# Swapping the stationary and the moving operand in the up, q/k/v and query products of a two-layer decoder trunk

## The chip, the cores and the metric

The kernel runs on one core of one Trainium2 chip. The metric is the device time of one execution in microseconds (us), as the median over several runs. A second number, the span, comes from one execution taken by the hardware profiler. Engines are named as the profile names them: PE is the matrix engine TensorE and PEld its weight loads, DVE is VectorE, ACT is ScalarE, POOL is GpSimd, and SP is the engine whose queue issues the weight transfers.

## The reference

x has 256 tokens of 2048 features, in float32. The trunk has two layers:

- Layer 1 is gated DeltaNet. `p = x @ w_in` gives q, k, v, a gate z and two scalars per head (16 heads of 128). A causal convolution of four taps and SiLU run over the tokens of each q/k/v channel; q and k are normalised per head, and a chunked delta rule (with a triangular solve) gives the heads' outputs, which are normalised, gated by SiLU(z) and multiplied by `w_out`.
- Layer 2 is differential attention. One product of the stream with `shared_w_kv` gives k and v; `x @ w_q` gives two query sets per head; the head's weights are softmax(1) - lambda * softmax(2); the result is normalised and multiplied by `w_o`.
- Each layer ends with an MLP, `square(relu(x @ w_up)) @ w_down`, with 8192 hidden features. After each of the four sub-layers comes `x <- LayerNorm(alpha * x + f(x))`.

Nearly all of the arithmetic is in the products of x (256 rows) with float32 weights, 421 MB of them in all, each read once.

## The kernel before

**Number format.** A float32 operand is split into a high and a low part of the type float32r: `split` (lines 77 to 79) copies the source into the high part on ScalarE (L78) and subtracts it on VectorE (L79). A product is then three matmuls, high x high, high x low and low x high, accumulated in PSUM (`product`, L174 to L176).

**Tiling of a product.** All big products go through `gemm`, which only puts an entry into a list, and `run`, which works the list off. A product of 1024 output columns (`C`) is cut along the depth into steps of four blocks of 128 (`SC`). For each depth block one transfer on SP's queue brings 128 rows of 1024 weights (512 KB, L159), and one split makes `wh` and `wl`. Inside a step, the kernel goes over two token tiles `t` of 128 tokens, over the depth blocks, and over two groups of 512 columns (`G`). The stationary operand is a 128 x 128 block of x (depth by tokens, `x_stat` or `act_stat`), the moving operand is 512 columns of weights, and the result is a PSUM bank of [128 tokens, 512 features]. After the first token tile of a step, the loads of the next step are emitted (L148 to L150), and after each token tile `pump` emits some units of queued head work.

**Transposes.** The next operation wants its operand with features on the partitions. So the evacuation of an up product (`up`, L341 to L350) takes Relu and square into a tile `sm` and queues `to_features` with `soon`. `run` takes one queued entry behind each depth block (L141 to L144): four transposes of 128 x 128 on TensorE (`transpose4`, L204), then a split out of PSUM. In the DeltaNet, q, k and v are evacuated into `sm` (L693), transposed and copied (`channels`, L499), since the convolution runs along the tokens of a channel. In the attention, `heads` does the same for k and q (L794, L798).

**Layout of x.** `xhl` (L61) holds x by features, as [128, part, token tile, depth block, 128 tokens].

**Order of the work.** The list is DeltaNet (k, q, v for the first eight heads, then for the others, two gate products, two output products), MLP, attention (k and q for the first eight heads, then for the others, two v products, two output products), MLP. An MLP goes through its 8192 hidden features in four quarters of 2048: two up products, then two down products onto the residual. Units of head work (convolutions, scores, the steps of the triangular inverse) are emitted by `pump` between the matmuls, in the order in which they were queued. After a LayerNorm the first products are cut [6, 5, 5] instead of [4, 4, 4, 4].

**Buffers.** Four raw weight tiles, six high and six low ones, eleven blocks of [128, 2048] (`blk`), eight small tiles (`sm`), and eight PSUM banks: four accumulators (`acc`) and four for everything else (`ps`).

## Time and profile before

| | |
|---|---|
| time, median of 3 runs | 2463.02 us (2461.49 to 2467.75) |
| time of the profiled execution | 2465.03 us |
| its span | 2463.3 us, mean clock of TensorE 0.992 |
| weight transfers on SP's queue | 420.79 MB, 52.0% of 16 DMA engines over the span |
| HBM read | 433.70 MB, 177 GB/s over the span |
| matmuls of 512 columns into `acc` | 9600 (3 lines x 3200) |
| transposes on L204 | 512 of `sm` tiles, 128 of `blk` tiles |

How to read a group row: line, engine, operation, output <- inputs, shape, count | busy time and mean duration of one in ns | idle time of that engine just before them, and what ended most of it. A row of a timeline is start, duration (both in us from the span's start), engine, line, operation, operands, count. A matmul's duration overlaps that of its neighbours, so the rate at which matmuls run is seen from their starts.

### The profile page before, as it was taken

Reading aid. Unit: us, or ns where it says so; the run is one execution under the profiler, and the core shown is the slowest. Engines: PE = TensorE matmul, PEld = TensorE weight load, DVE = VectorE, ACT = ScalarE, POOL = GpSimd, SP = SyncE. Lnnn points to the kernel's source line nnn. Section 1 sums busy time; section 2 is a strip of 40 time slices with the busy share of each in tenths; the row PEclk is TensorE's granted clock in tenths of the full one; section 3 lists DMA queues with packets and bytes.
Section 4 is the critical chain, followed back from the end, with each engine's and each line's share of the span. In section 5 each row is a group of like instructions: output and inputs, shape, how many; then the busy total and the mean of one; then the engine's idle time right before and its main releaser. Section 6 shows DMA issues by size and latency. Waiting matters only on the chain.

```text
span 2463.3 us, 30465 instructions
## 1 busy us (share of the span) xinstructions
PE 2416.1 (98%) x11492; PEld 1983.3 (81%) x11492; DVE 1497.2 (61%) x2333; ACT 1078.2 (44%) x1474; POOL 90.3 (4%) x94
## 2 busy tenths in 40 slices
PE   8999999998999999999998999999999999999997
PEld 7888888887888888888887878788788888888886
DVE  4789689667554544545557575665755554555556
ACT  4545345433443433434433464643443443443442
POOL 0010010002000000000002000000200000000001
PEclk9999899999999999999999999999999999999999
DMA  6545345564555556565554545455455555656553
GB/s 229 155 139 175 98 140 160 166 233 158 188 185 191 182 194 222 172 214 182 195 197 146 180 137 171 155 174 167 161 198 195 182 190 186 217 179 214 185 195 121
DMA packets 120211, 438.84 MB, mean 178 GB/s; under 512 B 13760, under 2 KB 13792, under 8 KB 119040
## 3 DMA queue, kind: packets, MB, share of 16 engines
q1 hardware_dynamic: 115920, 420.79, 52.0%
q0 software_dynamic: 2560, 11.13, 1.4%
q10 hardware_dynamic: 1584, 4.98, 0.5%
q8 instruction: 90, 1.47, 0.2%
q14 instruction: 57, 0.47, 0.1%
HBM read 433.70 MB, written 3.15 MB: 177 GB/s over the span
## 4 chain that ended last, share of the span: by engine, by line
PE 90%; DVE 6%; DMA 2%; issue 1%; ACT 1%; POOL 0%; ACTq 0%; POOLq 0%; DVEq 0%
PE acc L174 27%; PE acc L175 27%; PE acc L176 27%; PE ps L204 3%; DVE wl L79 1%; DVE blk L266 1%; DVE blk L265 1%; PE ps L819 1%; ACT wh L78 1%; PE ps L550 1%; DMA wr<-in_gdn_w_in_dram 1%; PE ps L485 1%; DMA wr<-in_mlp_w_up_dram 0%; PE ps L621 0%; PE ps L847 0%
## 5 line engine op out<-in xcount | busy, mean ns | idle before, releaser
L79 DVE TENSOR_TENSOR wl<-wr,wh 128x1024 fp32r<-128x1024 f32 x785 | 954.5, 1227 | 675.0 <-ACT wh L78 632.1
L78 ACT CAST wh<-wr 128x1024 fp32r<-128x1024 f32 x800 | 832.1, 1052 | 945.6 <-PE acc L176 757.2
L174 PE MATMUL acc<-wh,xhl 128*128 128x512 f32 x1920 | 764.3, 398 | 0.0
L175 PE MATMUL acc<-wl,xhl 128*128 128x512 f32 x1920 | 757.7, 395 | 3.2 <-POOL wl L79 3.2
L176 PE MATMUL acc<-wh,xhl 128*128 128x512 f32 x1920 | 754.8, 393 | 0.0
L174 PE MATMUL acc<-wh,blk 128*128 128x512 f32 x1280 | 500.0, 391 | 0.0
L176 PE MATMUL acc<-wh,blk 128*128 128x512 f32 x1280 | 499.4, 390 | 0.0
L175 PE MATMUL acc<-wl,blk 128*128 128x512 f32 x1280 | 499.1, 390 | 0.0
L175 PEld LDWEIGHTS acc<-wl,xhl 128*128 128x128 f32 x1920 | 363.7, 189 | 75.7 <-POOL wl L79 4.4
L174 PEld LDWEIGHTS acc<-wh,xhl 128*128 128x128 f32 x1920 | 363.8, 189 | 73.8 <-issue 1.7
L176 PEld LDWEIGHTS acc<-wh,xhl 128*128 128x128 f32 x1920 | 362.7, 189 | 73.9
L176 PEld LDWEIGHTS acc<-wh,blk 128*128 128x128 f32 x1280 | 240.4, 188 | 50.1
L174 PEld LDWEIGHTS acc<-wh,blk 128*128 128x128 f32 x1280 | 240.4, 188 | 49.5
L175 PEld LDWEIGHTS acc<-wl,blk 128*128 128x128 f32 x1280 | 240.5, 188 | 49.2
L293 DVE SCALAR_TENSOR_TENSOR blk<-blk,acc 128x512 f32<-128x512 f32 x80 | 54.7, 685 | 85.2 <-PE acc L176 85.2
L204 PE MATMUL ps<-ident,sm 128*128 128x128 f32 x512 | 81.3, 275 | 2.5 <-DVE sm L869 1.8
L204 PEld LDWEIGHTS ps<-ident,sm 128*128 128x128 f32 x512 | 61.3, 140 | 27.3 <-PE acc L176 7.1
L78 ACT CAST blk<-ps 128x512 fp32r<-128x512 f32 x80 | 46.8, 585 | 70.9 <-PE ps L204 70.9
L347 DVE TENSOR_TENSOR sm<-sm 128x512 f32<-128x512 f32 x64 | 44.0, 691 | 52.6 <-ACT sm L346 52.2
L79 DVE TENSOR_TENSOR blk<-ps,blk 128x512 fp32r<-128x512 f32 x80 | 55.0, 688 | 30.1 <-ACT blk L78 30.1
L346 ACT ACTIVATE sm<-acc 128x512 f32<-128x512 f32 x64 | 38.2, 597 | 65.4 <-PE acc L176 62.4
L471 DVE SCALAR_TENSOR_TENSOR sm<-blk,g_cw,sm 128x255 f32<-128x255 f32 (+2 forms) x144 | 60.8, 474 | 0.0
(202 smaller groups left out, 1049.7 us busy)
## 6 DMA issues: line engine op xcount, KB each, us to landing
wr<-in_mlp_w_up_dram SPq DMA_DIRECT2D x256, 512.0 KB, 4.7
wr<-in_mlp_w_down_dram SPq DMA_DIRECT2D x256, 512.0 KB, 5.2
wr<-in_gdn_w_in_dram SPq DMA_DIRECT2D x128, 512.0 KB, 4.4
wr<-in_shared_w_kv_dram SPq DMA_DIRECT2D x64, 512.0 KB, 5.1
wr<-in_gdn_w_out_dram SPq DMA_DIRECT2D x32, 512.0 KB, 5.4
wr<-in_diff_w_q_dram SPq DMA_DIRECT2D x32, 512.0 KB, 4.6
wr<-in_diff_w_o_dram SPq DMA_DIRECT2D x32, 512.0 KB, 4.7
blk<-in_ln_g_dram POOLq DMA_DIRECT2D x4, 1024.0 KB, 7.2
```

The costliest lines, as they stand in the source:

```text
L78: self.nc.scalar.copy(hi, src)
L79: (engine or self.nc.vector).tensor_tensor(lo, src, hi.bitcast(F32), op=ALU.subtract)
L174: mm(ps, xh, wh[:, c], start=(k == 0), stop=False)
L175: mm(ps, xh, wl[:, c], start=False, stop=False)
L176: self.last = mm(ps, xl, wh[:, c], start=False, stop=(k == nk - 1))
L204: self.nc.tensor.transpose(pt[:, i], src[:, i * P : (i + 1) * P], self.ident)
L265: v.scalar_tensor_tensor(xc, xc, ln["mv", t][:, 0:1], ln["g"][:, c], op0=ALU.subtract, op1=ALU.mult)
L266: v.scalar_tensor_tensor(xc, xc, ln["rs", t], ln["b"][:, c], op0=ALU.mult, op1=ALU.add)
L293: self.nc.vector.scalar_tensor_tensor(rc, rc, alpha, ps, op0=ALU.mult, op1=ALU.add)
L346: self.nc.scalar.activation(a, ps, AF.Relu)
L347: self.nc.vector.tensor_tensor(a, a, a, op=ALU.mult)
L471: v_.scalar_tensor_tensor(y[:, i, d:], u[:, : T - d], w(j), y[:, i, d:], op0=ALU.mult, op1=ALU.add)
```

## The change

Three families of products change their operands: up (all but the first 1024 columns of each MLP, which stay since they follow a LayerNorm), the DeltaNet's q/k/v, and the attention's queries and the second half of its keys. They go through a new list entry, `features`, of 512 output features. Now a 128 x 128 block of weights (depth by features) is stationary, x moves in passes of 256 columns (all tokens), and the result arrives as [128 features, 256 tokens]: four such blocks fill a pair of PSUM banks. No transposes follow; Relu, square and split (or the plain copies of q/k/v) work on the block as it is. Down, gate, v and output products stay as they were.

What goes with it: `xhl` and the activations become [128, depth block, part, 256 tokens], so that both token tiles stand next to each other; a weight transfer brings two depth blocks of 512 columns (runs of 2 KB) instead of one of 1024 (runs of 4 KB); a step covers eight depth blocks, with the same four transfers; the accumulators become two pairs of banks.

```diff
-        self.acc = pool("acc", 4, space=PSUM)
+        self.acc = pool("acc", 2, space=PSUM)
...
-        self.xhl = self.const.tile([P, 2, NT, KD, P], F32R, name="xhl")
+        self.xhl = self.const.tile([P, KD, 2, T], F32R, name="xhl")
...
+    def features(self, w, c0, evac, pre=None, rate=1):
+        wsrc = lambda k: w[k * P : (k + 2) * P, c0 : c0 + G].rearrange("(k p) c -> p k c", p=P)
+        self.plan.append((KD, wsrc, None, evac, pre, rate, None, [2 * SC] * (KD // (2 * SC))))
...
+            if stat is None:
+                if s == 0:
+                    acc = self.acc.tile([P, NG, G], F32, name="acc")
+                self.feature_passes(acc, ws, evac if s + n >= nk else None, lambda: self.load_next(loaded, steps, j), rate)
+                continue
...
+    def feature_passes(self, acc, ws, evac, load, rate):
+        blocks = acc.rearrange("p g (b t) -> p (g b) t", t=T)
+        mm = self.nc.tensor.matmul
+        for n, (k0, wh, wl) in enumerate(ws):
+            for i in range(2):
+                k = k0 + i
+                xh, xl = self.xhl[:, k, 0], self.xhl[:, k, 1]
+                for b in range(4):
+                    c = slice(i * G + b * P, i * G + (b + 1) * P)
+                    mm(blocks[:, b], wh[:, c], xh, start=(k == 0 and b % 2 == 0), stop=False, skip_group_check=True)
+                    mm(blocks[:, b], wh[:, c], xl, start=False, stop=False, skip_group_check=True)
+                    self.last = mm(
+                        blocks[:, b], wl[:, c], xh, start=False, stop=(k == KD - 1 and b % 2 == 1), skip_group_check=True
+                    )
+                if k != ws[0][0] and self.pending:
+                    fn, args = self.pending.popleft()
+                    with self.after(self.last):
+                        fn(*args)
+            if n == len(ws) // 2 - 1:
+                load()
+                self.pump(rate)
+        if evac is not None:
+            evac(blocks)
+        self.pump(rate)
...
-        for k in range(s, s + n):
+        for k in range(s, s + n, 2 if pairs else 1):
             wr = self.raw.tile([P, C], F32, name="wr")
-            self.nc.sync.dma_start(wr, wsrc(k))
+            self.nc.sync.dma_start(wr.rearrange("p (k c) -> p k c", k=2) if pairs else wr, wsrc(k))
...
-            if k == 0:
-                acc[g, t] = self.acc.tile([P, G], F32, name="acc")
+            if k == 0 and g == 0:
+                pair = self.acc.tile([P, NG, G], F32, name="acc")
+                acc.update({(i, t): pair[:, i] for i in range(NG)})
...
+            def up_features(blocks, h=h):
+                h.append(self.blk(F32R))
+                hv = self.act_view(h[-1])
+                a = [self.sm() for _ in range(2)]
+                for i in range(2):
+                    self.nc.scalar.activation(a[i], blocks[:, 2 * i : 2 * i + 2], AF.Relu)
+                for i in range(2):
+                    self.nc.vector.tensor_tensor(a[i], a[i], a[i], op=ALU.mult)
+                for i in range(2):
+                    kb = slice(2 * i, 2 * i + 2)
+                    self.split(hv[:, kb, 0], hv[:, kb, 1], a[i].rearrange("p (k q) -> p k q", k=2))
...
-            for n in range(FQ // C):
-                self.gemm(
-                    KD, self.cols(w_up, f * FQ + n * C), self.x_stat, up(n), cuts=[6, 5, 5] if f == n == 0 else None
-                )
+            first = C if f == 0 else 0
+            if first:
+                self.gemm(KD, self.cols(w_up, 0), self.x_stat, up(0), cuts=[6, 5, 5])
+            for c0 in range(first, FQ, G):
+                self.features(w_up, f * FQ + c0, up_features)
...
-            def ev_for(name, ct):
-                def ev(gi, t, ps):
-                    if (gi, t) == (0, 0):
+            def ev_for(name, ct, u):
+                def ev(blocks):
+                    if u == 0:
                         hf["raw"] = self.blk().rearrange("p (h t) -> p h t", h=HH)
-                    a = self.sm()
-                    nc.scalar.copy(a, ps)
-                    if (gi, t) == (NG - 1, NT - 1):
-                        turned(gi, t, a)
-                    else:
-                        self.soon(turned, gi, t, a)
...
+                    for h in (0, 2):
+                        nc.scalar.copy(hf["raw"][:, u * 4 + h : u * 4 + h + 2], blocks[:, h : h + 2])
+                    if u == 1:
                         follow()
...
-                self.gemm(KD, self.cols(w_in, c0 + H * DK), self.x_stat, ev_for(name, ct + H), pre=pre, rate=2)
+                for u in range(2):
+                    self.features(
+                        w_in, c0 + H * DK + u * G, ev_for(name, ct + H, u), pre=pre if u == 0 else None, rate=2
+                    )
...
-            return heads("q", follow)
+            for u in range(2):
+                self.features(w_q, hh * C + u * G, head_features("q", u, follow))
...
-            self.gemm(KD, self.cols(w_q, hh * C), self.x_stat, q_heads(hh))
+            if hh == 0:
+                self.gemm(KD, self.cols(w_kv, 0), self.x_stat, heads("k"), pre=constants, cuts=[6, 5, 5])
+            else:
+                for u in range(2):
+                    self.features(w_kv, C + u * G, head_features("k", u))
+            q_heads(hh)
```

`head_features` copies a block's four feature blocks into the heads' tile on ScalarE, as `ev` does for q/k/v. The gate scalars of the DeltaNet (L425, L426) read the new layout of x in the same matmuls.

More of the change, by code (lines that the diff above doesn't have):

```diff
@@ L147, in run, with load_next @@
                             evac(g, t, acc[g, t])
-                if t == 0 and j + 1 < len(steps):
-                    with self.after(self.hold):
-                        self.load_weights(loaded, *steps[j + 1], self.hold is not None)
-                    self.hold = None
+                if t == 0:
+                    self.load_next(loaded, steps, j)
                 self.pump(rate)
+    def load_next(self, loaded, steps, j):
+        if j + 1 < len(steps):
+            with self.after(self.hold):
+                self.load_weights(loaded, *steps[j + 1], self.hold is not None)
+            self.hold = None
@@ L161, in load_weights @@
             wl = self.lo.tile([P, C], F32R, name="wl")
-            self.split(wh, wl, wr, self.nc.gpsimd if share and k % 2 else None)
+            self.split(wh, wl, wr, self.nc.gpsimd if share and (k - s) // (2 if pairs else 1) % 2 else None)
             ws.append((k, wh, wl))
@@ L232, in turn @@
             with self.after(self.last):
-                self.to_features(r[t][:, cut(q)], self.xhl[:, :, :, q * 4 : q * 4 + 4], t)
+                self.to_features(r[t][:, cut(q)], self.xhl[:, q * 4 : q * 4 + 4], t)
         for c in (cut(0), slice(G, D)):
@@ L267, in ln_apply @@
         if ln["out"] is None:
-            self.to_features(xc, self.xhl[:, :, :, q * 4 : q * 4 + 4], t)
+            self.to_features(xc, self.xhl[:, q * 4 : q * 4 + 4], t)
         else:
@@ L420, in gates @@
             pg = self.ps()
[L421 removed]
+            pv2 = pg.rearrange("p (s q) -> p s q", s=2)
             for k in range(KD):
[L423 removed]
+                xk = self.xhl[:, k]
                 c = slice(k * P, (k + 1) * P)
[L425 to L426 removed]
+                nc.tensor.matmul(pv2, wh[:, c], xk, start=(k == 0), stop=False, skip_group_check=True)
+                nc.tensor.matmul(pv2[:, 0], wl[:, c], xk[:, 0], start=False, stop=(k == KD - 1), skip_group_check=True)
             gt = self.sm()
@@ L799, in turned, with head_features, ev @@
                 if follow is not None and (gi, t) == (NG - 1, NT - 1):
+                    follow()
+            return ev
+        def head_features(name, u, follow=None):
+            def ev(blocks):
+                if u == 0:
+                    st[name] = self.blk().rearrange("p (h t) -> p h t", h=8)
+                for h in (0, 2):
+                    nc.scalar.copy(st[name][:, u * 4 + h : u * 4 + h + 2], blocks[:, h : h + 2])
+                if follow is not None and u == 1:
                     follow()
```

24 lines of the change are left out of this document (6 added, 18 removed).

## The prediction

> **What bounds the kernel now.** I read the page first: engine shares, then the chain that ended last, then the costliest groups.
>
> ```profile
> span 2463.3 us, 30465 instructions
> ...
> PE 2416.1 (98%) x11492; PEld 1983.3 (81%) x11492; DVE 1497.2 (61%) x2333; ACT 1078.2 (44%) x1474; POOL 90.3 (4%) x94
> ...
> PE 90%; DVE 6%; DMA 2%; issue 1%; ACT 1%; POOL 0%; ACTq 0%; POOLq 0%; DVEq 0%
> ...
> L79 DVE TENSOR_TENSOR wl<-wr,wh 128x1024 fp32r<-128x1024 f32 x785 | 954.5, 1227 | 675.0 <-ACT wh L78 632.1
> L78 ACT CAST wh<-wr 128x1024 fp32r<-128x1024 f32 x800 | 832.1, 1052 | 945.6 <-PE acc L176 757.2
> L174 PE MATMUL acc<-wh,xhl 128*128 128x512 f32 x1920 | 764.3, 398 | 0.0
> ...
> L174 PE MATMUL acc<-wh,blk 128*128 128x512 f32 x1280 | 500.0, 391 | 0.0
> ...
> L204 PE MATMUL ps<-ident,sm 128*128 128x128 f32 x512 | 81.3, 275 | 2.5 <-DVE sm L869 1.8
> ...
> L78 ACT CAST blk<-ps 128x512 fp32r<-128x512 f32 x80 | 46.8, 585 | 70.9 <-PE ps L204 70.9
> L347 DVE TENSOR_TENSOR sm<-sm 128x512 f32<-128x512 f32 x64 | 44.0, 691 | 52.6 <-ACT sm L346 52.2
> L79 DVE TENSOR_TENSOR blk<-ps,blk 128x512 fp32r<-128x512 f32 x80 | 55.0, 688 | 30.1 <-ACT blk L78 30.1
> L346 ACT ACTIVATE sm<-acc 128x512 f32<-128x512 f32 x64 | 38.2, 597 | 65.4 <-PE acc L176 62.4
> ```
>
> TensorE is the bound: 90% of the chain, and its big matmuls idle 0.0 us before them. ScalarE (L78) and VectorE (L79), which split the weights, wait for TensorE (757.2 us of L78's idle time) and not the other way round. But a busy share says nothing of how long one matmul holds the engine, since neighbours overlap (398 ns each times 1920 is far more than their share). For that I cut one quarter of the last MLP (two up products of 1024 columns, then two down products of 1024) at its product borders and asked each stretch for its transposes alone; the columns are the stretch, its length, TensorE busy in L204 (count), weight loads (count), clock, DMA share, GB/s.
>
> ```profile
> 1915.28:1960.29 45.01, 1.82 (x12) 1.41 (x12) 1.00 0.57 187
> 1960.29:2005.80 45.51, 2.42 (x16) 1.90 (x16) 1.00 0.56 185
> 2005.80:2049.82 44.02, 0.60 (x4) 0.49 (x4) 1.00 0.59 192
> 2049.82:2093.34 43.52, 0.00 (x0) 0.00 (x0) 1.00 0.59 194
> ```
>
> The fourth product has no transpose and takes 43.52 us for its 192 matmuls of 512 columns (16 blocks of depth, 2 token tiles, 2 column groups, 3 terms): **226.7 ns each**, at the full clock. The other three exceed 43.52 by 1.49, 1.99 and 0.50 us and hold 3, 4 and 1 groups of four transposes. So 3.98 us over 8 groups: **0.497 us per group**, and nothing else in the quarter costs TensorE anything. The single events agree (start, duration):
>
> ```profile
> 628.38 0.39 PE L176 MATMUL acc<-wh,xhl 128*128 128x512 f32 x1
> 628.61 0.60 PE L204 MATMUL ps<-ident,sm 128*128 128x128 f32 x4
> 628.96 0.48 PE L174 MATMUL acc<-wh,xhl 128*128 128x512 f32 x1
> 629.28 0.40 PE L175 MATMUL acc<-wl,xhl 128*128 128x512 f32 x1
> 629.51 0.39 PE L176 MATMUL acc<-wh,xhl 128*128 128x512 f32 x1
> ```
>
> From L176 to the second matmul behind the group pass 0.90 us, 0.45 more than two matmuls; the rest of the 0.497 is in the following ones (here 0.23 instead of 0.227).
>
> **Which work is changed.** A block of 512 output features by 256 tokens was 96 matmuls of 512 columns (16 depths, 2 token tiles, 3 terms) and becomes 192 of 256 (16 depths, 4 feature blocks, 3 terms). Blocks that change: up, 14 in each of two MLPs (16 less the first 1024 columns) = 28; q/k/v of the DeltaNet, 6 products of 2 = 12; query products 2 of 2 = 4; the second key product 2. Together 46. So 4416 matmuls of 512 columns become 8832 of 256, the streamed columns are the same, and 4416 weight loads are added.
>
> **Removed: the transposes.** Each block loses 2 groups of four (one per token tile): 92 groups, 368 of the 512 in the L204 row. At 0.497 us: **-45.8 us**. The groups in the DeltaNet and attention stand between the same matmuls, so they get the same price; waits of TensorE for the copy ahead of a last group I leave at nothing.
>
> **Added: twice as many, half as long.** Break-even is easy to state: half of 226.7 is 113.3 ns, and 45.8 us over 8832 allow 5.2 ns more, so the change gains below **118.5 ns per pass** and loses above. The trace has few passes of 256 columns in the same number format (fp32r); these are a run of three on VectorE's scores, 16 of the gate columns, and for comparison the 512 ones:
>
> ```profile
> 347.99 0.28 PE L532 MATMUL ps<-sm,g_ones 128*128 128x256 f32 x1
> 348.11 0.28 PE L533 MATMUL ps<-sm,g_ones 128*128 128x256 f32 x1
> 348.22 0.28 PE L535 MATMUL ps<-sm,g_after 128*128 128x256 f32 x1
> 348.34 0.39 PE L551 MATMUL ps<-blk 128*128 128x128 f32 x2
> ```
>
> ```profile
> L426 PE MATMUL ps<-xhl,blk 128*128 128x256 f32 x16 | 4.5, 281 | 0.0
> ...
> L535 PE MATMUL ps<-sm,g_after 128*128 128x256 f32 x8 | 2.3, 283 | 0.0
> L533 PE MATMUL ps<-sm,g_ones 128*128 128x256 f32 x8 | 2.3, 282 | 0.0
> L532 PE MATMUL ps<-sm,g_ones 128*128 128x256 f32 x8 | 2.2, 280 | 0.0
> L534 PE MATMUL ps<-sm,g_after 128*128 128x256 f32 x8 | 2.2, 279 | 0.0
> ```
>
> Starts: 0.35 us over three passes, 117 ns. Durations: a 512 matmul lasts 391 ns (L174 on blk) and holds the engine 226.7, so 164 ns of a duration overlap the next; 279 to 283 less 164 give 115 to 119. Inside the run of three they rise (280, 282, 283), so a long stream should lie at the later ones: I take **118 ns**. Bounds: below, 113.3 (no pass can be had for less than its share of columns without beating the rate of the 512 ones); above, the 0.12 us between L535 and L551, say 121. Cost: 8832 x 4.7 = **+41.2 us** (0 to +67.7).
>
> The trace also shows why little slack is left. Eight weight loads with one-column matmuls take
>
> ```profile
> 144.59 0.99 PEld L485 LDWEIGHTS ps<-g_col,sm 128*128 128x128 f32 x8
> ```
>
> so (0.99 - 0.19 for the last one's own length) / 7 = 114 ns per load. Under a 512 matmul half of the time covers a load; under a pass of 256 all of it does.
>
> The Trainium skill ("TensorE: Matmul & The Clock Gate", section "Back-to-back issue gap") gives a warm gap of N/2.4 + 2.5 ns. That is 215.8 ns for 512 columns and 109.2 for 256, so each replaced matmul would cost only 2.5 ns more, 11 us in all. The trace disagrees on both sizes (226.7, and 117 to 118), so the measured rows go into my sum.
>
> **Moved: the evacuation.** Products now arrive transposed. Up's Relu, square and two-way split are as many instructions as before, read from SBUF instead of PSUM; DeltaNet loses its second ScalarE copy, the attention its VectorE copy. They run once per block instead of per token tile, on two PSUM banks while TensorE fills the other pair. Up's take 2 x 597 + 2 x 585 = 2.4 us on ScalarE and 2 x 691 + 2 x 688 = 2.8 us on VectorE, and a block lasts 192 x 118 = 22.7 us, so I cost them at nothing. The weight splits beside them are 8 of 1052 ns and 8 of 1227 per block, 8.4 and 9.8 us; if a block ran shorter than VectorE's 12.6 us, TensorE would wait for L79. The next step's loads are still issued from the middle of a step, behind them one pump of queued head work as before. Eight pumps per 1024 columns stay eight, so the order of the head work does not move. In products that stay as they were, an accumulator is now a pair of banks; the pair evacuated last is asked for again only in the second token tile of the next step, 24 x 0.227 = 5.4 us later. The very first step now needs two quarters of x instead of one, and the second is transposed by the pump in its middle, ahead of its use. Both at nothing.
>
> **Moved: the weight transfers.** Same number of transfers on SP's queue, same 512 KB, but in runs of 2 KB instead of 4 KB.
>
> ```profile
> wr<-in_mlp_w_up_dram SPq DMA_DIRECT2D x256, 512.0 KB, 4.7
> ...
> out_dram<-blk SPq DMA_DIRECT2D x5, 256.0 KB, 2.2
> ```
>
> The output rows are runs of 2 KB: 256 KB in 2.2 us against 512 KB in 4.7, no dearer per byte. A step of 11.3 us needs four transfers, which land while the step before it computes. I cost it at nothing; the other bound is rival three.
>
> **Sum.** -45.8 + 41.2 = -4.6 us on the profiled execution's 2465.0 (span 2463.3): 2460.4. That execution lay 2.0 us above the median of the runs, 2463.0, so I predict the median at **2458 us**, 0.2% less. About 0.3% (7.4 us) is what a measurement of this kernel can tell from no change, so the forecast is "hardly any change", with passes between 116.5 and 119.2 ns: -17.8 to +6.1 us, 2445 to 2469.
>
> **Rivals.**
> 1. *A pass costs exactly half* (113.3 ns): then the transposes are pure gain, -45.8 us, 2417. For it: in the fourth product above the 512 matmuls run at an even 226.7 when nothing else is mixed in, and the few 256 passes stand beside other forms. Against it: no 256 row reaches that, and the load takes 114 ns by itself. By the skill's gap, which speaks for this side, it would be -34.8.
> 2. *A matmul pays a fixed toll whatever its width* (the other side). If a long stream settles at the 0.12 us that lie between L535 and L551, two passes take 240.0 ns where one matmul took 226.7: 13.3 ns of toll for each matmul more, on TensorE in every changed block. That is 4416 x 13.3 = +58.7 us, less 45.8 = +12.9, **2476**. It decides from 118.5 ns. For it: the rising 280, 282, 283, the last of them at 119, and the load of 114 under each pass. Against it: L534, right behind a 512 matmul, lasts 279 (115).
> 3. *Weights come late.* If a 2 KB run took as long as a 4 KB one, the DMA share of 0.57 in an up product would become 1.14 and each of 46 blocks would stretch by 14% of 22.7 us: +146 us, about 2605. Against it, the output rows above.
>
> That the change doesn't do what it says, because a load's whole 0.19 us had to end between two passes, is excluded by the loads at 114 ns and the passes at 117.
>
> **How the numbers follow.** Forecast 0.62, rival 1 0.12, rival 2 0.24, rival 3 0.02. Faster by over 0.3% needs a pass under 117.7 ns: rival 1, and 0.43 of the forecast's band: 0.12 + 0.27 = 0.39. Within 0.3%: the rest of the band, 0.35. Slower: rivals 2 and 3, 0.26. The range reaches to 121 ns above (+21.9 us, 2484), and below to 114.6 ns (-34.6 us, 2428), which leaves out rival 1 at its purest and rival 3.
>
> **What would show it.** L204's sm row falls from 512 to 144. The new matmul rows, 2944 of each of three terms, last 282 ns on average (164 + 118); 277 speaks for rival 1, 284 or more for rival 2. The four products of the quarter above take 768 x 118 + 87.0 = 177.7 us instead of 178.06; 174.1 or 179.2 by the rivals. If TensorE idles ahead of new matmuls with L79 or L78 as releaser, or the DMA share in an up stretch is far above 0.6, my "nothing" for evacuation or transfers was wrong. If the passes take 118 and the time still moves by 20 us, what I left out lies in the DeltaNet or attention.

## The result, and the profile after

The changed kernel takes **2502.51 us** (median of 4 runs, 2500.04 to 2504.50), the kernel before in the same comparison 2465.39 us (4 runs, 2461.49 to 2480.45): ratio of the means **1.0139** (all ratios below are of means), 95% interval 1.0094 to 1.0183. It is slower by about 1.4%, above the range of the prediction (2428 to 2484). The profiled execution took 2500.82 us with a span of 2498.7 us, 35.4 us more than the span of before; its mean clock was 0.989 (0.992 before).

From the page of the changed kernel: the span, the engines' busy time, the shares of the chain that ended last, the costliest groups, the weight queue's share of the DMA engines, and the issues of up's weights (the last number is us to landing). By the new line numbers L182 to L184 are the three terms of the changed products, L219 to L221 those of the others, L79 and L80 the two instructions of a split, L249 the transposes.

```profile
span 2498.7 us, 38431 instructions
...
PE 2438.4 (98%) x15540; PEld 2186.9 (88%) x15540; DVE 1491.0 (60%) x2321; ACT 1062.8 (43%) x1450; POOL 88.6 (4%) x94
...
q1 hardware_dynamic: 163024, 420.79, 53.2%
...
PE 88%; DVE 7%; issue 2%; ACT 1%; DMA 1%; POOL 0%; SPq 0%; ACTq 0%; POOLq 0%; DVEq 0%
...
L182 PE MATMUL acc<-xhl,wh 128*128 128x256 f32 x2944 | 839.0, 285 | 7.0 <-ACT xhl L79 6.9
L183 PE MATMUL acc<-xhl,wh 128*128 128x256 f32 x2944 | 837.0, 284 | 1.8 <-DVE xhl L80 1.8
L184 PE MATMUL acc<-xhl,wl 128*128 128x256 f32 x2944 | 837.3, 284 | 0.0
...
L219 PE MATMUL acc<-wh,blk 128*128 128x512 f32 x1280 | 499.8, 391 | 3.7 <-DVE blk L339 3.7
...
wr<-in_mlp_w_up_dram SPq DMA_DIRECT2D x256, 512.0 KB, 4.2
```

TensorE still sets the end. The new rows have the forecast count, 2944 for each term, but last 284 to 285 ns, which the prediction had named as the sign of rival 2. The transfers in runs of 2 KB land as fast as before (4.2 us against 4.7), and nothing in the new rows waits for a weight split. The 6.9 us behind `xhl L79`, the 1.8 us behind `xhl L80` and the 3.7 us behind `blk L339` are waits that the kernel before did not have.

The timeline of the changed kernel inside an up product (start, duration in us) shows the pitch of the passes:

```profile
1991.77 0.28 PE L182 MATMUL acc<-xhl,wh 128*128 128x256 f32 x1
1991.89 0.28 PE L183 MATMUL acc<-xhl,wh 128*128 128x256 f32 x1
1992.01 0.28 PE L184 MATMUL acc<-xhl,wl 128*128 128x256 f32 x1
1992.13 0.28 PE L182 MATMUL acc<-xhl,wh 128*128 128x256 f32 x1
```

A pass every **0.12 us**. The same quarter of the last MLP as in the prediction (its second), cut at its four product borders (stretch, length, TensorE and weight loads in transposes, clock, DMA share, GB/s):

```profile
1945.43:1991.45 46.02, 0.00 (x0) 0.00 (x0) 1.00 0.70 206
1991.45:2037.53 46.08, 0.00 (x0) 0.00 (x0) 1.00 0.61 184
2037.53:2081.24 43.71, 0.00 (x0) 0.00 (x0) 1.00 0.51 169
2081.24:2124.93 43.69, 0.00 (x0) 0.00 (x0) 1.00 0.58 193
```

The two up products have no transposes left and take 384 passes x 120.0 = 46.08 us each, where 45.01 and 45.51 us included them. The down products, whose instructions did not change, take 43.69 us where the fourth took 43.52.

Cut at the products' borders over the whole trace, the stages are these (us):

| | first matmul | q/k/v | gate | output | MLP 1 | k, q, v | output | MLP 2 |
|---|---|---|---|---|---|---|---|---|
| before | 11.0 | 362.8 | 116.8 | 90.0 | 723.7 | 324.8 | 96.7 | 723.7 |
| changed | 13.6 | 373.4 | 122.2 | 93.1 | 731.6 | 324.5 | 97.3 | 729.3 |

### The profile page after: what moved, and what is told of

Read it like the earlier page. It is cut to its first block, busy times and chain, and to the rows that moved or that the text cites. A ratio compares the mean times of both kernels' runs of the same rounds, so it can differ in the third digit from the quotient of the medians.

```text
span 2498.7 us, 38431 instructions
## 1 busy us (share of the span) xinstructions
PE 2438.4 (98%) x15540; PEld 2186.9 (88%) x15540; DVE 1491.0 (60%) x2321; ACT 1062.8 (43%) x1450; POOL 88.6 (4%) x94
## 4 chain that ended last, share of the span: by engine, by line
PE 88%; DVE 7%; issue 2%; ACT 1%; DMA 1%; POOL 0%; SPq 0%; ACTq 0%; POOLq 0%; DVEq 0%
PE acc L219 14%; PE acc L182 14%; PE acc L220 14%; PE acc L221 14%; PE acc L183 14%; PE acc L184 14%; DVE wl L80 2%; PE ps L249 1%; PE ps L885 1%; ACT wh L79 1%; PE ps L607 1%; DVE blk L312 1%; DMA wr<-in_mlp_w_up_dram 1%; PE ps L545 1%; PE ps L678 0%
## 5 line engine op out<-in xcount | busy, mean ns | idle before, releaser
L80 DVE TENSOR_TENSOR wl<-wr,wh 128x1024 fp32r<-128x1024 f32 x785 | 963.8, 1233 | 769.1 <-ACT wh L79 744.5
L79 ACT CAST wh<-wr 128x1024 fp32r<-128x1024 f32 x800 | 833.7, 1050 | 1162.7 <-PE acc L221 542.7
L182 PE MATMUL acc<-xhl,wh 128*128 128x256 f32 x2944 | 839.0, 285 | 7.0 <-ACT xhl L79 6.9
L183 PE MATMUL acc<-xhl,wh 128*128 128x256 f32 x2944 | 837.0, 284 | 1.8 <-DVE xhl L80 1.8
L184 PE MATMUL acc<-xhl,wl 128*128 128x256 f32 x2944 | 837.3, 284 | 0.0
L182 PEld LDWEIGHTS acc<-xhl,wh 128*128 128x128 f32 x2944 | 567.6, 193 | 10.6 <-ACT xhl L79 7.8
L183 PEld LDWEIGHTS acc<-xhl,wh 128*128 128x128 f32 x2944 | 567.7, 193 | 3.2 <-DVE xhl L80 2.4
L184 PEld LDWEIGHTS acc<-xhl,wl 128*128 128x128 f32 x2944 | 567.5, 193 | 0.2
L219 PE MATMUL acc<-wh,blk 128*128 128x512 f32 x1280 | 499.8, 391 | 3.7 <-DVE blk L339 3.7
L221 PE MATMUL acc<-wh,blk 128*128 128x512 f32 x1280 | 498.5, 389 | 0.0
L219 PEld LDWEIGHTS acc<-wh,blk 128*128 128x128 f32 x1280 | 240.3, 188 | 57.5 <-DVE blk L339 8.3
L221 PEld LDWEIGHTS acc<-wh,blk 128*128 128x128 f32 x1280 | 240.3, 188 | 50.1
L220 PE MATMUL acc<-wl,xhl 128*128 128x512 f32 x448 | 179.5, 401 | 4.7 <-POOL wl L80 2.5
L219 PE MATMUL acc<-wh,xhl 128*128 128x512 f32 x448 | 181.1, 405 | 0.8 <-ACT wh L79 0.7
L221 PE MATMUL acc<-wh,xhl 128*128 128x512 f32 x448 | 179.0, 400 | 0.0
L220 PEld LDWEIGHTS acc<-wl,xhl 128*128 128x128 f32 x448 | 85.6, 191 | 24.2 <-POOL wl L80 4.6
L339 DVE SCALAR_TENSOR_TENSOR blk<-blk,acc 128x512 f32<-128x512 f32 x80 | 53.0, 683 | 89.1 <-PE acc L221 89.0
L219 PEld LDWEIGHTS acc<-wh,xhl 128*128 128x128 f32 x448 | 85.6, 191 | 20.6 <-ACT wh L79 2.1
L221 PEld LDWEIGHTS acc<-wh,xhl 128*128 128x128 f32 x448 | 85.5, 191 | 18.1 <-DVE xhl L80 0.9
```

Source lines behind the costliest of these rows:

```text
L79: self.nc.scalar.copy(hi, src)
L80: (engine or self.nc.vector).tensor_tensor(lo, src, hi.bitcast(F32), op=ALU.subtract)
L182: mm(blocks[:, b], wh[:, c], xh, start=(k == 0 and b % 2 == 0), stop=False, skip_group_check=True)
L183: mm(blocks[:, b], wh[:, c], xl, start=False, stop=False, skip_group_check=True)
L184: self.last = mm(blocks[:, b], wl[:, c], xh, start=False, stop=(k == KD - 1 and b % 2 == 1), skip_group_check=True)
L219: mm(ps, xh, wh[:, c], start=(k == 0), stop=False)
```

## Experiments

In the expectations, theory A is rival 2: every matmul pays a toll on top of its columns, and 120.0 ns is that of 256. A single run is read by its spans and stages, against the trace of before; medians and ratios stand where several rounds were run.

### The price of a pass

**Halves in the down products.** In the kernel before, each matmul of 512 columns in the down and output products becomes two of 256, each with its own load. Layout, transposes and buffers stay.

```diff
-            mm(ps, xh, wh[:, c], start=(k == 0), stop=False)
...
+            for i in range(2):
+                o, c = slice(i * T, (i + 1) * T), slice(g * G + i * T, g * G + (i + 1) * T)
+                mm(ps[:, o], xh, wh[:, c], start=(k == 0 and i == 0), stop=False, skip_group_check=True)
```

> The kernel before, where each matmul of 512 columns in the down and output products (3 x 1280 of them, activations stationary, weights streaming) is cut into two of 256 into the same bank. Nothing else changes: no layout, no transfer, no evacuation. Theory A, a fixed toll of 13.3 ns per matmul whatever its width: each pair costs 240.0 instead of 226.7 ns, 3840 x 13.3 = +51 us, span about 2514, durations of the halves 283 ns. Theory B, a pass costs its share of columns (113.3 ns): span as before, 2463. The prediction's 118 ns would give 3840 x 9.3 = +36 us, 2499.

Measured: span 2508.7 us, +45.4 where theory A gave +51; the MLPs 744.3 and 742.6, +20.6 and +18.9 us, for 3072 passes each (+20.5 by theory A). The rest of the gap lies where nothing was edited: the q/k/v stage took 357.4 us instead of 362.8, at a higher clock. From one half to the next, with nothing else between, pass 119.97 ns on average (7608 pitches). So the toll has nothing to do with which operand is stationary: cutting a matmul in two costs 13.3 ns.

**Widths of 384 and 128.** Is it a toll on any width, or a floor under short passes? In one kernel the down and output products stream only 384 of each 512 columns (a quarter of these products is left out); in the other each 512 is cut into four passes of 128.

```diff
+            if stat != self.x_stat:
+                ps, c = ps[:, :384], slice(g * G, g * G + 384)
```

> The kernel before, where the down and output products (3 x 1280 matmuls) compute 384 of each 512 columns and leave the other 128 columns out, so what they add to the residual is missing there. It gives a third width in a stream of equal matmuls. Theory A (columns/2.4 ns slope from 512 and 256, plus 13.3): 173.3 ns, duration about 337, 3840 x -53.3 = -205 us. Theory B (512 columns at 226.7 in proportion, and 256 held back to 120 by the weight load): 170.0 ns, -218 us.

```diff
+            for i in range(4):
+                o, c = slice(i * P, (i + 1) * P), slice(g * G + i * P, g * G + (i + 1) * P)
```

> The kernel before, with each matmul of 512 columns of the down and output products cut into four passes of 128 columns, each with its own weight load (15360 passes in place of 3840). If only columns / 2.4 + 13.3 ns counts, a pass takes 66.7 ns: 15360 x 66.7 - 870.5 = +154 us, 2619. If a weight load of 114 ns is the floor under a pass, 114 to 120 ns: +881 to +973 us, 3346 to 3438. If the floor is 120.0 ns, the passes of 256 columns stood on the same floor and not on the toll.

The timelines, first of the 384 kernel, then of the 128 one:

```profile
2089.83 0.33 PE L177 MATMUL acc<-wl,blk 128*128 128x384 f32 x1
2090.01 0.33 PE L178 MATMUL acc<-wh,blk 128*128 128x384 f32 x1
2090.18 0.33 PE L176 MATMUL acc<-wh,blk 128*128 128x384 f32 x1
2090.35 0.33 PE L177 MATMUL acc<-wl,blk 128*128 128x384 f32 x1
```

```profile
3300.01 0.28 PE L181 MATMUL acc<-wh,blk 128*128 128x128 f32 x1
3300.12 0.27 PE L182 MATMUL acc<-wl,blk 128*128 128x128 f32 x1
3300.23 0.28 PE L183 MATMUL acc<-wh,blk 128*128 128x128 f32 x1
3300.34 0.28 PE L181 MATMUL acc<-wh,blk 128*128 128x128 f32 x1
```

384 columns have a pitch of 173.3 ns (33.28 us for the 192 of a down product; the median of some 3800 pitches is 173), 128 columns one of 112. With 226.7 for 512 and 120.0 for 256, the three long widths lie on one line, **columns / 2.4 + 13.3 ns**; a floor of 120 with proportional lengths above it would have given 170.0 at 384. At 128 the line gives 66.7, and the measured 112 is close to the weight load (114 ns in the prediction's L485 row). So 256 columns still lie above the floor of the load, and 120.0 is the toll. The 128 kernel took 3643.32 us, beyond the upper 3438, since long stretches ran at a lower clock (mean 0.897): the second output product of the DeltaNet and that of the attention ran at 0.50 throughout and took 166.2 us each, 216 ns a pass, where most down products of the same size took 85.8 to 86.1 at 1.00. Why the clock fell in one and not in the other is open.

### The accumulators

**Only up changed.** q/k/v, queries and keys go back to the form of before.

```diff
-                for u in range(2):
-                    self.features(
-                        w_in, c0 + H * DK + u * G, ev_for(name, ct + H, u), pre=pre if u == 0 else None, rate=2
-                    )
+                self.gemm(KD, self.cols(w_in, c0 + H * DK), self.x_stat, ev_for(name, ct + H), pre=pre, rate=2)
```

> The changed kernel with the new operand order in the up products alone; DeltaNet and attention work as before. Theory A: 28 blocks, each 192 x 120.0 ns instead of 96 x 226.7 ns and two transpose groups of 497 ns, +0.286 us per block, +8 us: span about 2471, and the four products of a later MLP quarter 179.2 us. Prediction's 118 ns: -2.8 us, 2460, quarter 177.7 us. Theory C, that the rest of the loss belongs to the DeltaNet: its end (first up product) falls where it did before, at 580 us, and not at 602.

Measured: 2486.3 us, span 2484.6, some 14 us above theory A. The first up product starts at 586.1 us, between the 580 of theory C and the 602 of the changed kernel. The MLPs take 731.4 and 730.8 us, 7.7 and 7.1 more than before. Their toll less transposes is 14 blocks x (192 x 6.67 - 2 x 497 ns) = 4.0 us, so something else costs each of them more than 3 us.

**Only the pairs.** The kernel before, with nothing changed but its accumulators, two tiles of two banks instead of four of one.

```diff
-        self.acc = pool("acc", 4, space=PSUM)
+        self.acc = pool("acc", 2, space=PSUM)
...
+            if k == 0 and g == 0:
+                pair = self.acc.tile([P, NG, G], F32, name="acc")
+                acc.update({(i, t): pair[:, i] for i in range(NG)})
```

> The kernel before with one part of the change alone: the four accumulators of one bank become two pairs. The prediction costed that at nothing: output products of the DeltaNet 90.0 us, each MLP 723.7 us, as before. Rival (a pair is free only when both of its banks are evacuated, so matmuls wait at product borders): 1 us or more longer per MLP and 3 us in the DeltaNet's output products, as in the changed kernel.

Measured: span 2477.3, +14.0; the MLPs 727.3 and 727.9 (+3.6, +4.2), the DeltaNet's output 94.3 (+4.3), the other 97.6 (+0.9). The q/k/v stage (355.3, -7.5) and the gate stage (126.1, +9.3) moved more than these, and none of TensorE's waits for an evacuated pair (four, 3.7 us together) lies there. Nor is all of the rest the mechanism below: the DeltaNet's first output product is 3.7 us longer, at a mean clock of 0.96, and the first product of MLP 1 1.4 us, at 0.97. What repeats at every clock is 0.17 us at a down product and 0.6 to 1.2 us at the last product of a sub-layer. In the changed kernel the mechanism is seen at the last product, first on TensorE, then on VectorE (timeline, with the idle time before an instruction and what ended it):

```profile
2479.42 0.39 PE L221 MATMUL acc<-wh,blk 128*128 128x512 f32 x1
2480.73 0.50 PE L219 MATMUL acc<-wh,blk 128*128 128x512 f32 x1 [0.93 <-DVE blk L339]
```

```profile
2479.41 0.22 DVE L103 SCALAR_TENSOR_TENSOR rsq_t<-rsq_y,ln_rs 128x1 f32<-128x1 f32 x1
...
2479.99 0.68 DVE L339 SCALAR_TENSOR_TENSOR blk<-blk,acc 128x512 f32<-128x512 f32 x1
```

In the last step of a product the first column group of the second token tile is finished and evacuated (L339), then the second group goes on into the other bank of the same pair. As one tile, the pair is not written again before the evacuation has read it, so TensorE waits. At the ends of the four sub-layers TensorE waits 0.9 us each (the row's 3.7 us); elsewhere matmuls of the next product stand in between, and 0.17 us is left. How much of the 0.9 us counts in the end isn't shown: the waits for the LayerNorm behind it (`ps` of L249 behind `blk` of L312) are 9.1 us in all, where the kernel before waits 14.2.

The DeltaNet's first output product waits for something else. In the changed kernel (47.5 us against 45.0), VectorE and TensorE show:

```profile
513.81 0.23 DVE L833 TENSOR_SCALAR head_w<-head_w 128x128 f32<-128x128 f32 x1 [4.00 <-DMA head_w<-in_diff_subln_w_dram]
513.96 2.35 DVE L80 TENSOR_TENSOR wl<-wr,wh 128x1024 fp32r<-128x1024 f32 x2
515.23 0.50 PE L220 MATMUL acc<-wl,blk 128*128 128x512 f32 x1 [2.37 <-DVE wl L80]
```

The low part of a weight tile stands on VectorE behind an instruction that waits 4.00 us for the transfer of a small constant (`head_w`), and TensorE waits 2.37 us for it. The kernel with only the pairs shows the same (6.73 and 2.54 us), the kernel before no such wait of TensorE in this product.

**The changed kernel with one tile per bank.**

```diff
-                    acc = self.acc.tile([P, NG, G], F32, name="acc")
+                    acc = [self.acc.tile([P, G], F32, name="acc") for _ in range(NG)]
```

> The changed kernel with one accumulator tile per PSUM bank again (a feature block of 512 then holds two tiles of one bank); all passes as in the changed kernel. Theory (a pair is one tile, so the second column group of a row product's last step waits until the first has been evacuated): the pairs' cost goes, and an MLP takes 723.7 + 4.0 (560 passes' toll less the transposes) = 727.7 us instead of 731.6 and 729.3, the DeltaNet's output products 90 instead of 93.1; together about -9 us, near 2493 us. Rival (these stages are longer for another reason, such as the evacuations of feature blocks): MLPs stay at 731.6 and 729.3, and the time at 2502.

The first down product of the quarter shown above, and the last product of all (stretch, length, busy time and count of TensorE, of weight loads, of DVE, ACT and POOL, clock, DMA share, GB/s):

```profile
2040.70:2084.25 43.55, 43.55 (x194) 36.07 (x193) 21.31 (x21) 17.25 (x19) 0.00 (x0) 1.00 0.52 169
...
2442.70:2486.20 43.50, 43.50 (x193) 35.85 (x191) 25.64 (x35) 14.13 (x15) 2.27 (x2) 1.00 0.39 127
```

The same two took 43.71 and 44.78 us with pairs. Over the 18 output and down products that have no other work in them, the sum falls by some **5.6 us**; MLP 2 is at 727.4, as expected. The DeltaNet's output products came to 92.0, not to 90: the first of them still takes 47.0. The total did not fall, though 2493 was expected: 2504.67 us (4 runs), ratio 1.0151, 1.0120 to 1.0181. MLP 1 stays at 730.9 because its first product, behind a LayerNorm, grew from 56.96 to 58.19 (the waits for LayerNorms are back at 13.3 us), q/k/v grew to 379.0, and the mean clock was 0.985 instead of 0.989. What the clock is worth is seen below.

### The first step

**A finer first cut.** The first key block's step of eight depth blocks is cut into 4 and 4, so that its first matmuls need one quarter of x.

```diff
+                        cuts=[4, 4, 8] if hh == 0 and name == "k" and u == 0 else None,
```

> The changed kernel, whose very first block of 512 features is cut into steps of 4, 4 and 8 depth blocks instead of 8 and 8, so that the first step needs one quarter of x as before. Theory C (the start loses some 10 us because the second quarter of x is due within the first step, and its casts stand behind weight casts on ScalarE): 6 to 10 us less than the changed kernel, first step without a wait for xhl, no half clock at 26 to 33 us. Rival (transfers are late at the start, whoever waits): no difference beyond 2 us. Theory A leaves everything behind the first product as it is.

Why it was tried: in the changed kernel, the timeline of TensorE and ScalarE near the start has

```profile
22.75 1.03 PE L249 MATMUL ps<-ident,blk 128*128 128x128 f32 x8
...
23.93 1.04 ACT L79 CAST wh<-wr 128x1024 fp32r<-128x1024 f32 x1 [1.16 <-DMA wr<-in_gdn_w_in_dram]
...
27.24 1.06 ACT L79 CAST xhl<-ps 128x512 fp32r<-128x512 f32 x2
28.36 0.29 PEld L182 LDWEIGHTS acc<-xhl,wh 128*128 128x128 f32 x1 [4.82 <-ACT xhl L79]
28.36 0.58 PE L182 MATMUL acc<-xhl,wh 128*128 128x256 f32 x1 [4.58 <-ACT xhl L79]
```

The second quarter of x is transposed at 22.75, but its split stands on ScalarE behind casts of weights whose transfers arrive late (1.16 us of waiting for one of them). TensorE idles 4.58 us, and from the middle of this stall to 4.7 us behind it the clock is at half (windows of the changed kernel, columns as above):

```profile
26.30:33.10 6.80, 3.83 (x16) 3.54 (x17) 2.42 (x3) 2.01 (x3) 0.00 (x0) 0.50 0.78 262
33.10:74.90 41.80, 41.74 (x348) 41.30 (x347) 25.37 (x36) 18.70 (x23) 0.00 (x0) 1.00 0.53 152
```

By the Trainium skill ("TensorE: Matmul & The Clock Gate", section "What's actually happening") the gate knows only half and full and decides by windows of about 3.4 us; the trace agrees, with 0.50 for 6.80 us.

Measured: 2487.70 us (4 runs), ratio 1.0086 (1.0059 to 1.0112). q/k/v falls from 373.4 to 366.2 us, nearly all of it in the first key product, and the half clock at 26 us is gone. So the cut gave back **7.2 us**; by estimate 2.4 of them are the clock (half of the 4.7 us at half clock behind the stall). That 366.2 is also 362.8 plus the toll less transposes of the 12 blocks (12 x 0.286 = 3.4) is a coincidence. The page of this version still has waits for the splits of x,

```profile
L182 PE MATMUL acc<-xhl,wh 128*128 128x256 f32 x2944 | 840.7, 286 | 3.2 <-ACT xhl L79 3.2
L183 PE MATMUL acc<-xhl,wh 128*128 128x256 f32 x2944 | 838.1, 285 | 1.3 <-DVE xhl L80 1.3
```

4.5 us together, where the kernel before waits for none at the start, and the first key product takes 55.2 us against 50.4 before. What hides them is the fifth product of the stage, 77.1 us at a mean clock of 0.91 here, 80.7 at 0.87 before. The first matmul stayed late (13.4 against 11.0). What it takes to remove both stays open. The gate stage also fell, from 122.2 to 114.7, which the edit does not touch; that is the clock again:

```profile
427.00:494.30 67.30, 66.97 (x527) 55.78 (x525) 44.21 (x108) 29.14 (x64) 3.31 (x6) 1.00 0.41 134
```

is the second gate product here; in the changed kernel it is

```profile
434.40:509.10 74.70, 74.35 (x527) 61.65 (x525) 44.28 (x107) 29.18 (x64) 3.32 (x6) 0.89 0.38 120
```

The same 527 matmuls at 0.89 instead of 1.00 cost 7.4 us. It happens to any version: over all comparisons the kernel before took 2459.4 to 2462.9 us in its executions at a mean clock of 0.994, 2468.0 to 2471.5 at 0.990, 2472.2 to 2473.9 at 0.989 and 2478.9 to 2482.5 at 0.985 (one execution, 2473.4 us at 0.939, is out of line).

**Both repairs.** The finer first cut and one tile per bank together.

> The changed kernel with both repairs: the first key block cut into steps of 4, 4 and 8 depth blocks, and one accumulator tile per PSUM bank. Theory: what then stays is the toll of 8832 passes less the transposes, +13.1 us on 2463.3, and about 2.5 at the start: a span of 2479 us at a granted clock near 0.993, 2481 as a time (each 0.001 of clock is worth 1.6 to 2 us); the row products that pairs had lengthened take 43.55, 43.52, 43.52 us in the last quarter of the last MLP (43.71, 43.69 and 44.78 in the changed kernel), the q/k/v stage 366. Rival (the repairs overlap, or other costs of the new form remain): the span stays at the 2485 of the version with the cut alone.

Measured: 2493.68 us (4 runs), ratio 1.0074 (1.0050 to 1.0099), at clocks of 0.985 to 0.990. The execution at 0.990 took 2487.65, where the expectation gives 2481 + 3 x 1.8 = 2486; the profiled one, at 0.985, has a span of 2496.1. The products came as expected (43.55, 43.52, 43.52), and the first key product's two blocks and the next product took 111.7 us as with the cut alone (111.2; 118.1 without). q/k/v was 372.0, not 366: two products of it took 5.1 us more at clocks of 0.97 and 0.89. So the two repairs add up as far as one trace can show it. At 0.990 the loss left is 16 to 20 us (2487.65 against the 2468.0 to 2471.5 of before at that clock); the toll less transposes is 13.1 of it, the late first matmul about 2.

### Turning it round: fewer and longer passes

High and low part of x lie side by side, so `wh` can meet both in **one pass of 512 columns**, and only `wl` needs one of 256. The two halves of the result are then added by ScalarE and VectorE. The first key product stays as it was, with the finer first cut.

```diff
+                    mm(acc[:, b], wh[:, c], xk, start=(k == 0), stop=False, skip_group_check=True)
+                    self.last = mm(
+                        acc[:, b, :T], wl[:, c], xk[:, :T], start=False, stop=(k == KD - 1), skip_group_check=True
+                    )
```

> The changed kernel with first_cut, where (all but the first key product) the two matmuls that share a weight block become one: weights stationary, high and low part of x side by side as 512 streaming columns into a whole bank, then 256 columns of low weights times high x into its first half; ScalarE copies the second half and VectorE adds the first. Blocks are of 256 features, transfers have runs of 1 KB. Theory A: 226.7 + 120.0 = 346.7 ns instead of 3 x 120.0 per weight block, 64 weight blocks in each of 44 blocks: 44 x 64 x 13.3 = -37.5 us against first_cut, about 2455, a little faster than before. Theory B (no toll, the loss comes from elsewhere): same as first_cut.

Measured: 2476.21 us (10 runs), ratio 1.0036 (1.0018 to 1.0053): better, but more than half of the expected gain is missing (the span fell by 16.8 us against the finer first cut alone, not by 37.5). The timeline shows why:

```profile
999.65 0.40 PE L142 MATMUL acc<-xhl,wh 128*128 128x512 f32 x1
999.88 0.28 PE L143 MATMUL acc<-xhl,wl 128*128 128x256 f32 x1
1000.00 0.40 PE L142 MATMUL acc<-xhl,wh 128*128 128x512 f32 x1
1000.24 0.28 PE L143 MATMUL acc<-xhl,wl 128*128 128x256 f32 x1
1000.36 0.40 PE L142 MATMUL acc<-xhl,wh 128*128 128x512 f32 x1
```

A pair takes 353.9 ns (236.0 + 117.9), not 226.7 + 120.0 = 346.7. Alternating widths cost 7.2 ns more per pair, 20.3 us over the 2816 pairs. So the two kinds were put into separate runs of eight:

```diff
+            for i in range(4):
+                k = k0 + i
+                for b in range(2):
+                    c = slice(i * T + b * P, i * T + (b + 1) * P)
+                    self.last = mm(
+                        acc[:, b, :T], wl[:, c], self.xhl[:, k, 0], start=False, stop=(k == KD - 1), skip_group_check=True
+                    )
```

> The kernel wide, where within each weight tile the eight matmuls of 512 columns come first and the eight of 256 after them, instead of alternating. Same matmuls, same transfers, same evacuation. Theory A2 (a stream of equal matmuls settles at its columns plus 13.3 ns, 226.7 and 120.0; an alternating one does not settle, 353.9 ns per pair in wide): a tile takes 8 x 346.7 instead of 8 x 353.9 ns, 88 blocks of 4 tiles, 58 ns each: -20 us against wide, a little below before. Theory A1 (the price of a pair is what it is, whatever the order): no difference from wide.

Measured: 2463.03 us (12 runs), ratio 0.9970 (0.9949 to 0.9990); the MLPs are at 721.4 and 720.6, under the 723.7 of before. Part of the gain over before is the clock: at 0.993 four executions took 2461.0 to 2462.7 us, those of before 2462.7 to 2466.0. The passes are not quite back at 226.7 and 120.0 (timeline, a run of eight of each kind merged):

```profile
1001.13 2.00 PE L142 MATMUL acc<-xhl,wh 128*128 128x512 f32 x8
1002.97 1.11 PE L151 MATMUL acc<-xhl,wl 128*128 128x256 f32 x8
1003.92 0.40 PE L142 MATMUL acc<-xhl,wh 128*128 128x512 f32 x1
```

Eight long passes take 1.84 us, 230 ns each, and eight short ones 0.95, 119 each: 349 a pair. By the medians over some 350 such runs, the long passes start with pitches of 233, 236, 228, 233 and 231 ns and are at 227 from the sixth on; the short ones start with 113 and 119 and are at 120 from the third on. A stream needs a few passes to settle. With the first key product as in the kernel before, on top of it:

```diff
+                if not hh and name == "k":
+                    self.gemm(KD, self.cols(w_in, c0 + H * DK), self.x_stat, ev_rows(name, ct + H), pre=pre, rate=2)
```

> wide_grouped with the very first key product done as in the kernel before (x stationary, transposes after it). Theory C (the start loses because the new order needs x of both token tiles before its first matmul and a step covers more depth): first matmul at 11.0 instead of 12.9 us, 3 to 8 us less than wide_grouped, about 2445 to 2450, 0.5 to 0.8% below before. Rival (the start costs only what the transposes spared give back): no difference.

Measured: 2467.31 us (12 runs), ratio 0.9987 (0.9969 to 1.0005). The first matmul came at 11.4 instead of 12.9, but q/k/v took 358.1 instead of 353.4, so in all the saving did not show. In this trace the clock covers it: the first two products took 108.7 us instead of 110.3, so that 3 us are gained at their end, and the fifth took 75.0 at a clock of 0.91 instead of 70.0 at 1.00. Whether the start is worth the expected 3 to 8 us stays open. Last, the grouped version with one tile per bank:

> The grouped wide version (high and low part of x as one pass of 512 columns, the low part of the weights in passes of 256, the two kinds in separate runs), with one accumulator tile per PSUM bank. Theory: a block of 512 features takes 64 x 226.7 + 64 x 120.0 = 22.19 us, before it took 96 x 226.7 + 2 x 497 ns = 22.76; so 14 blocks give an MLP of 723.7 - 8.0 = 715.7 us instead of the 721.4 and 720.6 of the version with pairs, the output products of the DeltaNet 90 instead of 95.5, in all some -17 us against it: about 2446 us, ratio to before 0.992. Rival (the pairs cost nothing in this version, or the smaller evacuations cost as much): MLPs stay near 721, 2463 us, ratio 0.997.

Measured: **2457.49 us** (12 runs, 2443.13 to 2467.98), ratio **0.9961** (0.9938 to 0.9985), the fastest of all. The DeltaNet's output products are at 90.3 as expected, the MLPs at 721.1 and 718.1 instead of 715.7: the two up products of a quarter take 44.67 and 44.69 us where 128 x 226.7 + 128 x 120.0 is 44.4 (the passes that have not settled, again), and MLP 1's first product 58.15 instead of 54.97. At equal clock (0.994) three executions took 2444.4 to 2446.3 us, where the kernel before took 2459.4 to 2462.9; its median lies higher since eight of its twelve executions ran at 0.985 to 0.990.

## Why the prediction was wrong

Two steps failed: the price of a pass, which turned the sign, and the terms put at nothing, which took the result out of the range. The working against what the traces show, in us of span:

| term | forecast | measured |
|---|---|---|
| 92 groups of transposes | -45.8 | -45.8 (count measured, price of before) |
| 8832 passes | +41.2 (118 ns) | +58.9 (120.0 ns) |
| the very first step | 0 | +2.6 at the start, +7.2 by the finer cut, +4.5 of waits left with it |
| accumulators in pairs | 0 | +5.6 |
| weight split behind `head_w` | not priced | +2.4 |
| gate stage at a lower clock | not priced | +5.4 |
| fifth q/k/v product, clock 0.91 instead of 0.87 | not priced | -3.9 (-3.4 measured, with 0.6 of toll in it) |
| unassigned | | -1.5 |
| sum | -4.6 | +35.4 |

- **The price of a pass** ("I take 118 ns") was the term that turned the sign. The break-even of 118.5 held; the stream settled at 120.0, above it, by the mechanism, the place and nearly the size of rival 2 (toll less transposes +13.1, there +12.9). The clue was quoted: 280, 282, 283 ns in a run of three, and 0.12 us behind the last. A run of three had not settled, as the grouped version shows (113, 119, then 120 behind longer passes, 117 on average), and the forecast stopped between its mean and its end. With 120.0 alone the sum would have been 2476, still inside the range. The overlap of 164 ns, taken from 512 columns, did carry over: 284 less 164 is 120.
- **The toll itself** could have been read from the 512 columns. By the Trainium skill ("TensorE: Matmul & The Clock Gate", section "Back-to-back issue gap") an isolated gap is N/2.4 + 2.5 ns; the row gave 226.7, which is N/2.4 + 13.3. The prediction saw the disagreement and used the page for rival 1 only; kept as a toll per matmul, with the measured 13.3, the same form gives 120.0 at 256 and 173.3 at 384, and the runs agree.
- **"The very first step ... Both at nothing"** was wrong about the first: the pump does transpose the second quarter ahead of its use, but its split then queues on ScalarE behind casts that wait for weights. The prediction asked when the transposes are issued, not what stands ahead of their evacuation. The finer cut gave back 7.2 us; the 4.5 us of waits that it leaves and the 2.6 us at the start have no experiment of their own.
- **The pairs** were costed by when a pair is next asked for. What costs time is inside the pair: one bank is read while the other is still to be written. The 5.6 us are a sum over products; that the whole time falls by as much isn't shown.
- **Right:** the count of transposes (L249's `sm` row has 144), the transfers in runs of 2 KB (rival 3 falls), the evacuation and the weight splits, which hold up none of the new matmuls, and the quarter as a test: 179.50 us against 177.7, 174.1 and 179.2 by forecast, rival 1 and rival 2.
- **The range** held the unknown price of a pass, but no bound for the terms costed at nothing. This is what put the result outside it: these terms are 19.9 of the 35.4 us, and the rows that were not priced 3.9.
- **The clock.** The mean clock varies between executions of one version, and in the traces of the versions the stretches at half clock lie in different products of the DeltaNet. That the gate stage's +5.4 belongs to the change isn't shown, nor the -3.9; what sets the clock there was not settled. At a mean clock of 0.990 the changed kernel took 2500.04 us and the kernel before 2468.0 to 2471.5, so 29 to 32 us of the loss are there at equal clock.

## What to carry to other kernels

Price a cut of matmuls by a toll per matmul read from the long ones (here 226.7 less 512/2.4), not from a short run of the new size, which has not settled. An edit costed at nothing needs a bound like any other: look for what stands ahead of it on the engine that it moves to, and for tiles that get a reader while part of them is still to be written. Where two products share a stationary operand, stream them as one long pass, and keep passes of one width together, in runs of more than a few. Compare versions that differ by less than 1% at equal clock, and where the sum of a stage closes exactly, look at its products one by one: two terms may hide each other.

## What the runs showed of the hardware

- A float32r stream with a load per matmul runs at columns / 2.4 + 13.3 ns: 226.7, 173.3 and 120.0 ns for 512, 384 and 256 columns. At 128 it is 112, the pace of the weight loads.
- Passes of 512 and 256 in turn take 353.9 ns a pair, in runs of eight of a kind 349, and 346.7 by the rates that long streams settle at.
- A stall of 4.58 us of TensorE at the start comes with 6.8 us at half the clock, of which 4.7 lie behind it, so its price is not its length alone: the cut that removed it gave 7.2 us.
